# Full-row low pass in C's scores and A's compressed product, batched fronts in D, and a new order of the attention in a hybrid mixer layer

## The chip, the cores and the metric

The kernel runs on one core of one Trainium2 chip. The metric is the device time of one execution in microseconds; times are given as the median of several runs. A core has five engines with queues of their own: TensorE (PE, matrix products; its weight loads are listed as PEld), VectorE (DVE), ScalarE (ACT), GpSimd (POOL) and SyncE (SP, which here only issues DMAs). PSUM has eight banks of 128 rows by 512 numbers of 32 bits, into which PE writes.

## What is computed

One layer: a normalised and modulated input `h` of 1024 tokens by 1024 channels, projections of it, four causal token mixers of four heads of 64 channels each, gated products with `w_br`, a sum over the mixers with gates taken from `h`, an output projection with residual, and a last RMSNorm.

```python
shift, scale, gate = split(silu(c) @ w_ada + b_ada, 3)
h = rms_norm(x, norm_g) * (1 + scale) + shift
(a_q, a_kv, a_g, a_z, b_q, b_k, b_v, b_z,
 c_q, c_k, c_v, c_z, d_q, d_k, d_v, d_z) = split(h @ w_in)
y_a = nsa_attention(a_q, a_kv, a_g, ...)      # compressed, full and window parts
y_b = banded_attention(b_q, b_k, b_v, 128, slopes, sink)
y_c = stick_breaking_attention(c_q, c_k, c_v)
y_d = retention(d_q, d_k, d_v)
for y, z in branches:
    merged += sigmoid(h @ w_merge[i]) * ((y * silu(z)) @ w_br[i])
x = x + gate * (merged @ w_out)
out = rms_norm(x, final_g)
```

For C the score `z` of a query and a key runs over 64 channels, and its weight is `exp(log_sigmoid(z) + suffix)`, with `suffix` the sum of `log_sigmoid(-z)` over the keys between. For D, chunks of 128 tokens have a product of queries and keys times a decay matrix, and a state of 64x64 numbers for each head is carried from chunk to chunk. A's compressed part has 32 keys, each made from a block of 32 tokens.

## The kernel before, in words

**Exact parts.** Most matmuls take operands of a short type (F32R). So that the product keeps its precision, an operand is split in two parts, high and low (`hh`, `hl` of the input, `whi`, `wlo` of weights, `hi`, `lo` of attention weights), and a dense product is three matmuls: `hh·whi`, `hl·whi`, `hh·wlo`. A head has 64 channels, so for C's scores the high and low parts of a query stand one above the other in 128 rows (`q_item`: [hi; lo] for the first head of a pair, [lo; hi] for the second), and the high part of the keys stands twice, in both halves of rows (`ck_item`, L556; the second copy by a DMA on SP). One matmul over 128 rows then gives (q_hi + q_lo)·k_hi. A second one, over the 64 rows of q_hi, adds q_hi·k_lo (`c_units`, L1153 and L1154); the low parts of both heads' keys share one tile `klo`, the first head's in its upper half of rows and the second's in the lower. Matmuls of D's mixer and the transposes are in full 32 bits.

**Stages.** 0 to about 75 us: the norm, the modulation, the first tiles of projections. Then attention by groups: C0a and C0b (C's first two heads, in two parts), D0, C1, D1, A0, A1, B0, B1, to about 600 us. From 600 to 1000 us the merge, whose gate projections are done in Winograd's form (sums and differences `tt` of blocks of `h`, and of weights), and then the output projection with the norms. A group is a row of units. A unit of C is one head and two blocks of 128 queries; a unit of D (`d_units`, L1190) one chunk of 128 tokens for two heads; A and B take a block of queries. Each unit has a `front` (scores, in banks `s`, and what makes weights of them) and a `back` (transposes into banks `t`, the split in `hi` and `lo`, products with values into `y`; `pv_blocks`, L1078). In between run the dense projection items, in banks `d`, which fill PE.

**Buffers.** PSUM: three banks `s`, two `t`, two `d`, one `y`. `sp_pool` has four places of 128x1024 for rows of weights, `t1_pool` two of 128x512, and the weight loads `wst` two. A C front takes two places of `sp_pool`. D's front in the kernel before keeps its products in a place of `t1_pool`.

**What sets the order.** The class `Program` notes every instruction in plain program order with a rank. `SHIFT_PE` and `SHIFT` (L99, L111) add numbers to the ranks of whole parts, named by group and unit, such as ("C1", 2) or ("item", 21). `schedule()` (L256) is then a list schedule of the five engines with durations from `cost()` (L172): each engine takes, of what should be ready, the instruction of lowest rank. `issue()` emits them in that order, which is why nearly all instructions carry line L304 in the trace. The order on each engine is fixed when the program is built; at run time an engine waits until its next instruction's inputs are there.

**In D's front**, for each chunk: two score matmuls with 64 rows (head 0 on rows 0 to 63, head 1 on rows 64 to 127) into two banks, a transpose of the keys, two products with the decay matrix on DVE (128x128), two scalings on ACT, one product of the queries with the decay `xi` on POOL.

Of the kernel before, what the change touches and what calls it, by code (L numbers as in the profile page):

```python
# [10 lines left out]
F32 = mybir.dt.float32  # L11
# [18 lines left out]
# columns of w_in  # L30
# [68 lines left out]
SHIFT_PE = {  # L99
# [7 lines left out]
    ("h1", 7): -10600, ("item", 2): -80, ("item", 4): -11000, ("item", 5): -9200, ("item", 9): 9800, ("item", 11): 0,  # L107
    ("item", 16): -10000, ("item", 21): 9800, ("item", 23): 14100, ("item", 26): 13200, ("item", 27): 19300,
    ("item", 28): 2200, ("item", 30): 12600, ("mod", 5): -11400, ("mod", 6): -9700,
}  # L110
SHIFT = {  # L111
# [8 lines left out]
    ("item", 2): 12700, ("item", 3): 14900, ("item", 4): 10000, ("item", 7): 10200, ("item", 12): -13400, ("item", 13): 9500,  # L120
    ("item", 15): -10000, ("item", 16): 13100, ("item", 18): -8700, ("item", 19): 9600, ("item", 22): 10000,
    ("item", 23): 9800, ("item", 24): 9700, ("item", 25): -10100, ("item", 27): -800, ("item", 29): 12700, ("mod", 4): 10000,
    ("mod", 6): 10100, ("split", 5): 9400, ("x", 4): -10000,
# [4 lines left out]
class Op:  # L128
    __slots__ = ("eng", "calls", "dur", "lat", "preds", "succs", "prio", "start", "step", "size")

    def __init__(self, eng, prio, step):
        self.eng, self.prio, self.step = eng, prio, step
        self.calls, self.dur, self.lat, self.size = [], 0.0, 0.0, 0
        self.preds, self.succs = set(), []


class Program:
    """Instructions are first noted in plain program order, then issued by a list schedule of all engines: each
    engine takes, of what should be ready, the instruction that comes first by rank."""
# [17 lines left out]
    # -- noting  # L157
# [14 lines left out]
    def cost(self, eng, name, out, ins, kw):  # L172
# [16 lines left out]
        if eng == "dve":  # L189
# [4 lines left out]
            if name == "tensor_tensor_reduce":  # L194
                return 77 + n * 1.042
# [10 lines left out]
    def note(self, eng, name, fn, args, kw):  # L206
# [48 lines left out]
    # -- issuing  # L255
    def schedule(self):  # L256
# [6 lines left out]
        engs = ("pe", "act", "dve", "pool", "sp")  # L263
# [8 lines left out]
        dma = warm = 0.0  # L272
        while len(order) < len(ops):
# [5 lines left out]
            op = ops[i]  # L279
            op.start = t  # L280
# [26 lines left out]
    def noted(self, tc, late=0.0):  # L307
        """a part of the program whose instructions are noted, then issued; the other engines come to it later than TensorE"""
# [24 lines left out]
class Pool:  # L333
    """Slots that the tiles of a tag take in turn."""
# [12 lines left out]
class Slots:  # L347
    """Places that tiles take in turn."""
# [10 lines left out]
def hybrid_kernel(ctx: ExitStack, tc: tile.TileContext, x, c, w_ada, b_ada, norm_g, w_in, cmp_pos,  # L359
# [21 lines left out]
    # ------------------------------------------------------------ weights  # L381
# [6 lines left out]
    class Loads:  # L388
        """Loads run two pieces ahead of their splits."""
# [42 lines left out]
    def mtile_weights(it, srcs):  # L432
        """srcs: ((dram view [P, KC, n], n), ...) that make up 128 columns"""
# [33 lines left out]
    def mm3(ps, hi, lo, n0):  # L467
        """ps += h^T-projection of a 128-column weight tile for 512 tokens, in exact parts"""
# [7 lines left out]
    # ------------------------------------------------------------ prologue  # L476
# [12 lines left out]
    vcr = cst.tile([64, P], F32R, name="vcr")  # L489
# [13 lines left out]
    # ---------------------------------------------------- dense items  # L503
# [24 lines left out]
    def half_item(col, full):  # L528
        """the second half of the tokens of an item whose first half is there"""
# [12 lines left out]
    def q_item(col, q0, q1, scale, load=True):  # L542
        """query pair -> stacks [hi; lo] of the first head, [lo; hi] of the second"""
# [12 lines left out]
    def ck_item(col, kk0, kk1, klo, load=True):  # L556
        def evac(ps, n):
# [5 lines left out]
            ve.tensor_tensor(klo()[0:64, sl], ps[0:64], kk0()[0:64, sl].bitcast(F32), ALU.subtract)  # L563
            ve.tensor_tensor(klo()[64:128, sl], ps[64:128], kk1()[64:128, sl].bitcast(F32), ALU.subtract)
# [15 lines left out]
    def v_item(col, vout, tmp, is_d, load=True):  # L580
        """values of a head pair: channel-major projection, turned token-major on chip"""
# [26 lines left out]
    def z_item(col, br, p):  # L608
        """y *= 2 silu(z); all but the first branch of the merge wait in DRAM for their turn"""
# [22 lines left out]
    CK = [(2, 3, 4), (9, 10, 11)]  # L632
# [11 lines left out]
    for p in range(2):  # L644
        it_c.append([q_item(C_Q + P * p, rs(CQ[p][0]), rs(CQ[p][1]), 0.125, False),
                     ck_item(C_K + P * p, rs(CK[p][0]), rs(CK[p][1]), rs(CK[p][2]), False),
                     v_item(C_V + P * p, (lambda p: lambda: R["v2"](CV[p]))(p), Fs[1 + 2 * p], False, False)])
# [54 lines left out]
    # compression of keys and values of A: both at once through block-diagonal weights; the exact parts of the rows stand  # L702
    # side by side as one stationary operand, those of the weights as one moving operand
# [3 lines left out]
    def w1_split(h):  # L707
        """sixteen of the 32 rows of a block, four to a slot"""
# [29 lines left out]
    def cmp_done(g):  # L738
# [29 lines left out]
        te.matmul(pv[0:32, 0:64], lhsT=sg[64:128], rhs=w2t[64:128], start=True, stop=True)  # L768
        kkc, llc = R["q"]["kc"], R["q"]["lc"]
# [18 lines left out]
    # the first tiles grow along with the modulation: one row block of weights after the other  # L788
# [20 lines left out]
    # the second half of the tokens  # L809
# [61 lines left out]
    # pieces follow the order of the items  # L871
# [15 lines left out]
    # ---------------------------------------------------------------- attention  # L887
    with ac:
# [20 lines left out]
        # the compressed keys stand before those of the full part  # L909
# [4 lines left out]
        R["kcs"], R["lcs"] = RAF[:, 0:S + 32], RAF[:, S + 32:2 * S + 64]  # L914
        R["zz"] = RW
# [1018 lines left out]
```

## Time and profile before

| what | value |
|---|---|
| runs of the kernel before | 1148.17, 1146.26, 1146.23 us; median 1146.26 |
| profiled execution: span (it has no other time) | 1143.8 us, 16113 instructions |
| PE busy | 1076.6 us, 94% |
| PEld busy (weight loads, beside PE) | 879.8 us, 77% |
| DVE busy | 841.2 us, 74% |
| ACT busy | 591.6 us, 52% |
| POOL busy | 597.7 us, 52% |

The span runs from the first to the last instruction that the profiler recorded. Matmuls overlap in the records: each has a start and a modelled end, so the cost of one in a run is read from its start to the next start. In the names of a row, `d<-hh,whi` is a matmul into bank `d` of `hh` with weights `whi`; `128*128 128x512` are rows and columns of the stationary operand, then the moving operand. RA, RV, RW and RQ are large tiles that are used as slots for the stacks of queries, keys and values, FA the one for full 32-bit rows. PEclk is the share of full clock that PE was granted.

### The profile page before, as it was taken

What the parts mean: (1) busy time and instruction counts of PE and PEld (TensorE: products, weight loads), DVE (VectorE), ACT (ScalarE), POOL (GpSimd) and SP (SyncE); (2) the same over time, 40 slices, a digit from 0 to 9 for tenths busy, and PEclk for the clock granted to TensorE, in tenths of its full rate; (3) what the DMA queues carried; (4) which work ended last, traced back from release to release, by engine and by line L of the source; (5) the groups of instructions that cost most, each with busy time, mean ns of one, the idle gap of its engine ahead of it and who ended that gap; (6) DMA issues with size and microseconds to landing.
All of it is one profiled execution on the core that took longest, in us unless ns stands there. A gap on an engine that the chain in (4) does not pass through costs nothing. (4 is left out here: it accounts for less than half of the span.)

```text
span 1143.8 us, 16113 instructions
## 1 busy us (share of the span) xinstructions
PE 1076.6 (94%) x5391; PEld 879.8 (77%) x5391; DVE 841.2 (74%) x1777; ACT 591.6 (52%) x1317; POOL 597.7 (52%) x598
## 2 busy tenths in 40 slices
PE   5899999999999999999999589999999999988984
PEld 3777787688888888888878468887778888866763
DVE  6969975887557777767778995666686565678887
ACT  4388863886347666666763333422333333344343
POOL 4683215211535455454455653456666666776775
PEclk9899999999999999999999799999999999998998
DMA  9843102113022010013022023322222332332221
GB/s 300 243 127 84 47 1 52 43 37 56 14 75 55 10 47 29 28 37 76 29 75 69 33 60 95 99 78 65 78 88 56 52 98 73 119 111 87 80 92 74
DMA packets 119591, 85.03 MB, mean 74 GB/s; under 512 B 14428, under 2 KB 107668, under 8 KB 119508
## 3 DMA queue, kind: packets, MB, share of 16 engines
q1 hardware_dynamic: 118352, 80.55, 24.6%
q0 software_dynamic: 1088, 3.43, 0.8%
q8 instruction: 42, 0.69, 0.2%
q14 instruction: 41, 0.34, 0.1%
q10 hardware_dynamic: 68, 0.02, 0.0%
HBM read 72.45 MB, written 8.39 MB: 71 GB/s over the span
## 5 line engine op out<-in xcount | busy, mean ns | idle before, releaser
L304 POOL TENSOR_TENSOR wlo<-wst,whi 128x512 fp32r<-128x512 f32 (+1 forms) x108 | 141.8, 1324 | 176.0 <-ACT whi L304 173.8
L304 PE MATMUL d<-hh,whi 128*128 128x512 f32 x440 | 186.5, 424 | 3.1 <-ACT whi L304 2.5
L304 PE MATMUL d<-hh,wlo 128*128 128x512 f32 x440 | 174.9, 398 | 2.6 <-DVE wlo L304 2.6
L304 PE MATMUL d<-hl,whi 128*128 128x512 f32 x440 | 173.9, 396 | 0.0
L304 ACT ACTIVATE whi<-wst 128x512 fp32r<-128x512 f32 (+2 forms) x121 | 89.1, 736 | 104.7 <-DMA wst<-in_w_merge_dram 41.9
L304 PEld LDWEIGHTS d<-hh,wlo 128*128 128x128 f32 x440 | 83.7, 190 | 21.8 <-DVE wlo L304 3.0
L304 PEld LDWEIGHTS d<-hh,whi 128*128 128x128 f32 x440 | 84.0, 191 | 20.4 <-issue 4.0
L304 ACT ACTIVATE hi<-t 128x512 fp32r<-128x512 f32 (+3 forms) x148 | 74.7, 526 | 46.3 <-PE t L304 38.6
L304 PEld LDWEIGHTS d<-hl,whi 128*128 128x128 f32 x440 | 84.2, 191 | 10.5 <-POOL hl L304 0.2
L304 POOL TENSOR_SCALAR SP<-SP,den,gates 128x640 f32<-128x640 f32 (+7 forms) x64 | 49.7, 786 | 81.4 <-DVE den L304 61.5
L304 DVE TENSOR_TENSOR lo<-t,hi 128x512 fp32r<-128x512 f32 (+2 forms) x132 | 79.9, 621 | 10.5 <-ACT hi L304 9.7
L304 PE MATMUL s<-hl,whi 128*128 128x512 f32 x200 | 79.2, 397 | 3.4 <-DVE hl L304 3.4
L304 PE MATMUL s<-hh,wlo 128*128 128x512 f32 x200 | 79.5, 398 | 1.9 <-DVE wlo L304 1.9
L304 PE MATMUL s<-hh,whi 128*128 128x512 f32 x200 | 80.2, 401 | 0.1
L304 PE MATMUL t<-kbt,SP 128*128 128x128 f32 (+1 forms) x470 | 69.0, 275 | 8.3 <-DMA kbt<-in_kb_dram 7.0
L304 ACT ACTIVATE SP<-SP,mx 128x257 f32<-128x257 f32 (+9 forms) x96 | 62.3, 650 | 22.8 <-DVE mx L304 18.0
L304 ACT ACTIVATE mt<-mt 128x512 f32<-128x512 f32 x56 | 35.0, 625 | 69.9 <-POOL mt L304 50.2
L304 POOL TENSOR_TENSOR acc<-acc,mt 128x512 f32<-128x512 f32 x44 | 67.7, 1539 | 6.1 <-DVE mt L304 6.1
L304 PEld LDWEIGHTS t<-kbt,SP 128*128 128x128 f32 (+1 forms) x470 | 54.7, 141 | 17.9 <-DMA kbt<-in_kb_dram 7.0
L304 POOL TENSOR_TENSOR mt<-mt,mt 128x512 f32<-128x512 f32 x34 | 52.4, 1540 | 12.6 <-DVE mt L304 11.8
L304 PE MATMUL s<-tt,whi 128*128 128x512 f32 x176 | 54.5, 391 | 0.0
L304 PE MATMUL s<-RA,RW 128*128 128x256 f32 (+13 forms) x216 | 49.8, 332 | 0.3 <-DMA RA<-RA 0.3
(360 smaller groups left out, 2961.4 us busy)
## 6 DMA issues: line engine op xcount, KB each, us to landing
wst<-in_w_merge_dram SPq DMA_DIRECT2D x32, 512.0 KB, 4.4
wst<-in_w_in_dram SPq DMA_DIRECT2D x26, 512.0 KB, 3.7
FA<-in_w_ada_dram SPq DMA_DIRECT2D x10, 512.0 KB, 7.5
FA<-in_x_dram SPq DMA_DIRECT2D x8, 512.0 KB, 4.5
pst<-in_w_br_dram SPq DMA_DIRECT2D x32, 128.0 KB, 2.2
ga<-in_w_ada_dram SPq DMA_DIRECT2D x16, 256.0 KB, 3.0
wr<-in_w_out_dram SPq DMA_DIRECT2D x4, 1024.0 KB, 7.5
z<-in_x_dram SPq DMA_DIRECT2D x8, 512.0 KB, 3.5
```

Source lines behind the costliest of these rows:

```text
L304: fn(*args, **kw)
```

## The change

Four things.

1. **C's low pass.** The second matmul of a score takes all 128 rows, q's high and low parts, against the keys' low part, which now has to stand in both halves of rows, in a tile of its own for each head. For the first head pair two more DMAs on SP for each half of the tokens make the second copy. For the second pair the low parts go to a spare slot "f2", and four DMAs on POOL's queue copy them into the slots 2 and 3, which held the first pair's keys. There are 24 such matmuls for each head pair, of 128 to 512 columns. The product q_lo·k_lo is added by this.
2. **A's compressed product.** The matmul with the compressed values `vcr` takes 128 rows in place of 64; rows 64 to 127 of `vcr` are zeroed by a memset on POOL. There are 16, of 256 columns.
3. **D's fronts** are done for four chunks at once, in every fourth unit: eight two-head score matmuls in a row, four transposes, two DVE products of 128x512 in place of eight of 128x128, two ACT instructions in place of eight, one POOL product of 128x512 in place of four. The results stand in two places of `sp_pool` in place of one of `t1_pool`.
4. **The order.** Both tables of numbers are new throughout, and the planner's costs change: other factors for matmuls, 300 ns more for an operation on PE that has a stationary operand of 64 rows or less, and DVE and POOL not at once where both use a port. The order of the merge and the output comes from these costs too. Comments are dropped.

```diff
 SHIFT_PE = {
-    ("A0", 2): 600, ("A0", 4): 100, ("A0", 6): -9300, ("A0", 7): 10000, ("A0", 10): 10500, ("A0", 11): -10000,
+    ('A0', 0): -10000, ('A0', 1): 1967, ('A0', 11): -300, ('A0', 12): -10000, ('A0', 13): 0,
...
             if "rhs" in kw and m.dtype == F32:
-                return max(214.0, n * 1.668)
-            return 2.5 + max(104.5, n * 0.4167)
+                return max(214.0, n * (1.63 if kw["lhsT"].shape[0] <= 64 else 3.33))
+            return max(109.0, n * 0.4427)
...
+            wide = [a for a in ins if a.shape[-1] > 1 and str(a.space) == "SB"]
+            n = 2 - (name in ("tensor_copy", "tensor_scalar") and str(out.space) == "SB")
+            op.port |= eng == "pool" and bool(ins) or eng == "dve" and len(wide) >= n
+            if eng == "pe" and "lhsT" in kw and kw["lhsT"].shape[0] <= 64 and not op.narrow:
+                op.narrow = True
+                op.dur += 300.0
...
+            if op.port:
+                t = max(t, port["dve" if e == "pool" else "pool"])
+                port[e] = t + op.dur
...
-    vcr = cst.tile([64, P], F32R, name="vcr")
+    vcr = cst.tile([P, P], F32R, name="vcr")
...
-    def ck_item(col, kk0, kk1, klo, load=True):
+    def ck_item(col, kk0, kk1, kl0, kl1, both, load=True):
...
-            ve.tensor_tensor(klo()[0:64, sl], ps[0:64], kk0()[0:64, sl].bitcast(F32), ALU.subtract)
-            ve.tensor_tensor(klo()[64:128, sl], ps[64:128], kk1()[64:128, sl].bitcast(F32), ALU.subtract)
+            ve.tensor_tensor(kl0()[0:64, sl], ps[0:64], kk0()[0:64, sl].bitcast(F32), ALU.subtract)
+            ve.tensor_tensor(kl1()[64:128, sl], ps[64:128], kk1()[64:128, sl].bitcast(F32), ALU.subtract)
+            if both:
+                sy.dma_start(kl0()[64:128, sl].bitcast(F32), kl0()[0:64, sl].bitcast(F32))
+                sy.dma_start(kl1()[0:64, sl].bitcast(F32), kl1()[64:128, sl].bitcast(F32))
...
-    CK = [(2, 3, 4), (9, 10, 11)]
+    CK = [(2, 3, 4, 11), (9, 10, "f2", "f2")]
+    CKL = [(4, 11), (2, 3)]
...
-                     v_item(D_V + P * p, lambda: DV3, Fs[2 + p], True)])
+                     v_item(D_V + P * p, lambda: DV3, Fs[1 + 2 * p], True)])
...
+        po.memset(vcr[64:128].bitcast(F32), 0.0)
...
-                        te.matmul(y[:, yc:yc + n], lhsT=v, rhs=hi[:2 * nk, col:col + n], start=f, stop=end)
+                        te.matmul(y[:, yc:yc + n], lhsT=v, rhs=hi[:, col:col + n], start=f, stop=end)
...
-            klo = slot(CK[p][2])
+            klo = [slot(i) for i in CKL[p]]
+            if p == 1:
+                for e in range(2):
+                    for o in (slice(0, 64), slice(64, 128)):
+                        po.dma_start(klo[e][o], slot(CK[p][2])[64 * e:64 * e + 64])
...
-                                te.matmul(ps[:, :n], lhsT=q[hr], rhs=klo[hr, c0:c0 + n], start=False, stop=True)
+                                te.matmul(ps[:, :n], lhsT=q, rhs=klo[e][:, c0:c0 + n], start=False, stop=True)
...
+                    if n % 4:
+                        res["w"] = four["w"]
+                        return
...
-                    for e in range(2):
-                        b = slice(64 * e, 64 * e + 64)
-                        te.matmul(sp[e][:, 0:P], lhsT=DK[b, bl], rhs=DQ[b, bl], start=True, stop=True)
+                    for c in range(4):
+                        for e in range(2):
+                            b = slice(64 * e, 64 * e + 64)
+                            te.matmul(sp[e][:, c * P:(c + 1) * P], lhsT=DK[b, cs[c]], rhs=DQ[b, cs[c]], start=True, stop=True)
```

What the order does is read from the listing of each engine's instructions, before (L304) and changed (L346). The first place is PE, at D0's first fronts, where the scores are `s<-FA`. Before:

```order
L304 MATMUL d_131<-hh,wlo_141 128x512
L304 MATMUL s_132<-FA 128x128
L304 MATMUL s_133<-FA 128x128
L304 MATMUL t_139<-kbt,SP 128x128 x4
L304 MATMUL t_125<-kbt,SP 128x128 x4
L304 MATMUL d_131<-kbt,FA 128x128 x4
L304 MATMUL s_132<-FA 128x128
L304 MATMUL s_133<-FA 128x128
```

The same place changed:

```order
L346 MATMUL d_130<-hh,wlo_137 128x512
L346 MATMUL d_131<-kbt,FA 128x128 x4
L346 MATMUL s_132<-FA 128x128
L346 MATMUL s_133<-FA 128x128
L346 MATMUL s_132<-FA 128x128
L346 MATMUL s_133<-FA 128x128
```

A pair of scores stood between transposes or dense work each time; now four pairs (two are shown) stand in a run.

The second place is POOL behind the first tiles, where splits of weights (`wlo<-wst,whi`) meet the copies of C1's keys (`RA<-FA`) and D0's product (`SP<-FA`; before `t_127<-FA`). Before:

```order
L304 TENSOR_TENSOR wlo_137<-wst_124,whi_136 128x512 x2
L304 TENSOR_TENSOR wlo_141<-wst_138,whi_140 128x512 x2
L304 TENSOR_TENSOR t_127<-FA 128x128 x2
L304 TENSOR_TENSOR t_129<-FA 128x128
L304 TENSOR_SCALAR rs_157<-mv_156 128x2
```

Changed:

```order
L346 TENSOR_TENSOR wlo_137<-wst_124,whi_136 128x512 x2
L346 DMA RA<-FA 64x1024 x2
L346 TENSOR_TENSOR wlo_141<-wst_138,whi_140 128x512 x2
L346 TENSOR_TENSOR SP<-FA 128x512
L346 DMA RA<-FA 64x1024 x2
L346 TENSOR_TENSOR SP<-FA 128x512
L346 TENSOR_SCALAR rs_157<-mv_156 128x2
```

The four copies are new, in two pairs (one for each slot), each ahead of other work of POOL; D0's products are done in two.

The third place is DVE at the start of the merge, where `mt` and `tt` are sums of blocks of the input and `ga` sums for the output's gate. Before:

```order
L304 TENSOR_TENSOR mt_5763<-hh 128x512
L304 TENSOR_TENSOR mt_5766<-hh 128x512
L304 TENSOR_SCALAR ga_5770<-ga_5769,silc 128x128
L304 TENSOR_TENSOR mt_5763<-mt_5763,mt_5764 128x512
L304 SCALAR_TENSOR_TENSOR ga_5770<-ga_5769,silc,ga_5770 128x128
L304 TENSOR_TENSOR mt_5765<-hh,mt_5763 128x512
L304 TENSOR_TENSOR tt<-mt_5763,tt 128x512
```

Changed:

```order
L346 TENSOR_TENSOR mt_5712<-hh 128x512
L346 TENSOR_TENSOR mt_5715<-hh 128x512
L346 TENSOR_TENSOR mt_5712<-mt_5712,mt_5713 128x512
L346 TENSOR_TENSOR mt_5715<-mt_5715,mt_5716 128x512
L346 TENSOR_TENSOR tt<-mt_5712,tt 128x512
L346 TENSOR_TENSOR mt_5714<-hh,mt_5712 128x512
L346 TENSOR_TENSOR tt<-mt_5715,tt 128x512
```

The gate sums are gone from here, and two chains of block sums alternate. The first sum of weights for the next products (`s<-wst`) is the 20th row behind the first one shown before, and the 33rd changed.

## Rows read from the trace of the kernel before

**Rows 1.** The page: busy us, share of the span, instructions of each engine.

```profile
PE 1076.6 (94%) x5391; PEld 879.8 (77%) x5391; DVE 841.2 (74%) x1777; ACT 591.6 (52%) x1317; POOL 597.7 (52%) x598
```

**Rows 2.** Busy time by stage, whole kernel; the first line names the columns.

```profile
core 0: us, PE busy (x) PEld busy (x) DVE busy (x) ACT busy (x) POOL busy (x), PEclk, DMA share, GB/s
75.00:152.00 77.00, 77.00 (x367) 58.04 (x368) 69.57 (x131) 67.02 (x141) 25.08 (x18) 1.00 0.24 65
...
192.00:267.00 75.00, 73.36 (x386) 56.66 (x387) 62.40 (x130) 59.89 (x136) 15.93 (x17) 1.00 0.19 41
267.00:600.00 333.00, 329.82 (x1986) 284.41 (x1985) 235.17 (x814) 206.34 (x553) 160.44 (x239) 1.00 0.17 44
600.00:690.00 90.00, 74.99 (x298) 58.73 (x297) 81.31 (x93) 31.12 (x57) 51.23 (x39) 0.91 0.19 59
```

**Rows 3.** Waits of PE, 75 to 600 us: total us, times, longest.

```profile
PE y L304 <- DVE FA L304: 1.7, 2, 1.3
...
PE y L304 <- DVE yt L304: 0.4, 1, 0.4
```

**Rows 4.** Timeline of PE in C0: start us, us, instruction, count.

```profile
108.36 0.59 PE L304 MATMUL s<-RA,RW 128*128 128x256 f32 x2
108.88 0.50 PE L304 MATMUL d<-hh,whi 128*128 128x512 f32 x1
109.21 0.39 PE L304 MATMUL d<-hl,whi 128*128 128x512 f32 x1
...
111.50 0.81 PE L304 MATMUL s<-RA,RW 128*128 128x512 f32 x2
112.24 0.55 PE L304 MATMUL t<-kbt,SP 128*128 128x128 f32 x3
```

**Rows 5.** Timeline of PE in A: a score of two full-row matmuls.

```profile
488.30 0.46 PE L304 MATMUL s<-RA,RQ 128*128 128x320 f32 x2
488.60 0.39 PE L304 MATMUL d<-hh,whi 128*128 128x512 f32 x1
488.83 0.40 PE L304 MATMUL d<-hl,whi 128*128 128x512 f32 x1
```

**Rows 6.** Busy time in 100 to 125 us, columns as in rows 2.

```profile
100.00:125.00 25.00, 25.00 (x122) 18.92 (x121) 23.70 (x44) 22.48 (x48) 5.07 (x5) 1.00 0.20 54
```

**Rows 7.** Timeline of PE in A: the compressed product and its neighbours.

```profile
486.99 0.28 PE L304 MATMUL y<-lo,RV 128*128 128x256 f32 x1
487.19 0.38 PE L304 MATMUL y<-hi,vcr 64*128 64x256 f32 x1
487.50 0.50 PE L304 MATMUL d<-hh,whi 128*128 128x512 f32 x1
487.84 0.39 PE L304 MATMUL d<-hl,whi 128*128 128x512 f32 x1
```

**Rows 8.** Groups by line and shape: count, busy us, mean ns.

```profile
L304 PE MATMUL y<-hi,vcr 64*128 64x256 f32 x16 | 6.1, 381 | 0.1
```

**Rows 9.** Timeline of PE in D0: one front's scores.

```profile
155.09 0.28 PE L304 MATMUL y<-lo,RA 128*128 128x256 f32 x1
155.29 0.49 PE L304 MATMUL s<-FA 64*128 64x128 f32 x4
155.72 0.50 PE L304 MATMUL d<-hh,whi 128*128 128x512 f32 x1
156.06 0.39 PE L304 MATMUL d<-hl,whi 128*128 128x512 f32 x1
```

**Rows 10.** DMA issues: count, KB each, median us from issue to landing.

```profile
yd<-FA POOLq DMA_DIRECT2D x12, 256.0 KB, 2.4
...
RA<-RA SPq DMA_DIRECT2D x20, 128.0 KB, 2.2
```

**Rows 11.** Waits of PE, 600 to 690 us, columns as in rows 3.

```profile
PE d L304 <- ACT whi L304: 5.4, 1, 5.4
```

More of the change, by code (lines that the diff above doesn't have):

```diff
@@ L99 @@
 SHIFT_PE = {
[7 rows of a table removed]
-    ("h1", 7): -10600, ("item", 2): -80, ("item", 4): -11000, ("item", 5): -9200, ("item", 9): 9800, ("item", 11): 0,
-    ("item", 16): -10000, ("item", 21): 9800, ("item", 23): 14100, ("item", 26): 13200, ("item", 27): 19300,
-    ("item", 28): 2200, ("item", 30): 12600, ("mod", 5): -11400, ("mod", 6): -9700,
[12 rows of a table added]
+    ('first', 0): 300, ('first', 1): 0, ('first', 2): 300, ('first', 4): 9970, ('first', 5): 21923,
[3 rows of a table added]
+    ('h1', 7): 0, ('item', 0): 0, ('item', 10): 0, ('item', 11): 43, ('item', 12): 0,
@@ L110 @@
+    ('item', 13): 100, ('item', 14): -100, ('item', 16): -9900, ('item', 17): 10870,
+    ('item', 19): 9990, ('item', 2): -10000, ('item', 21): 0, ('item', 22): 0, ('item', 26): 633,
+    ('item', 28): 10000, ('item', 30): 9997, ('item', 4): -300, ('item', 5): 9997,
+    ('item', 6): 9960, ('item', 7): 9967, ('item', 9): 2077, ('mod', 0): 0, ('mod', 1): 3000,
+    ('mod', 2): 11000, ('mod', 3): 2900, ('mod', 4): -11000, ('mod', 5): -3, ('mod', 6): 0,
+    ('mod', 7): 7000,
 }
 SHIFT = {
[8 rows of a table removed]
-    ("item", 2): 12700, ("item", 3): 14900, ("item", 4): 10000, ("item", 7): 10200, ("item", 12): -13400, ("item", 13): 9500,
@@ L121 @@
-    ("item", 15): -10000, ("item", 16): 13100, ("item", 18): -8700, ("item", 19): 9600, ("item", 22): 10000,
-    ("item", 23): 9800, ("item", 24): 9700, ("item", 25): -10100, ("item", 27): -800, ("item", 29): 12700, ("mod", 4): 10000,
-    ("mod", 6): 10100, ("split", 5): 9400, ("x", 4): -10000,
[12 rows of a table added]
+    ('D1', 5): 10173, ('D1', 6): 2990, ('ada', 3): -300, ('ada', 4): 10000, ('ada', 7): -30,
[3 rows of a table added]
+    ('item', 1): 10300, ('item', 10): -9910, ('item', 12): 20, ('item', 13): -10320,
+    ('item', 14): -300, ('item', 15): -10997, ('item', 16): 9997, ('item', 18): 0,
@@ new lines @@
+    ('item', 19): 1100, ('item', 2): 0, ('item', 20): 0, ('item', 21): 0, ('item', 22): 273,
+    ('item', 23): 0, ('item', 24): 100, ('item', 25): -10000, ('item', 26): 19676, ('item', 27): 0,
+    ('item', 28): -9700, ('item', 29): -10000, ('item', 3): -3000, ('item', 30): 997,
+    ('item', 4): 130, ('item', 5): 0, ('item', 6): 0, ('item', 7): 0, ('item', 8): -10643,
+    ('item', 9): -10000, ('mod', 1): -11000, ('mod', 3): 0, ('mod', 4): 1000, ('mod', 5): -10800,
+    ('mod', 6): -10980, ('mod', 7): -10000, ('split', 0): 0, ('split', 1): -10000,
@@ L124 @@
+    ('split', 2): -3000, ('split', 3): -10000, ('split', 4): -200, ('split', 6): 10300,
+    ('split', 7): 21169, ('x', 4): 19990, ('x', 5): 10300, ('x', 6): 0, ('x', 7): -10000,
 }
@@ L128 @@
 class Op:
-    __slots__ = ("eng", "calls", "dur", "lat", "preds", "succs", "prio", "start", "step", "size")
+    __slots__ = ("eng", "calls", "dur", "lat", "preds", "succs", "prio", "start", "step", "size", "port", "narrow")
     def __init__(self, eng, prio, step):
@@ L133, in __init__ @@
         self.calls, self.dur, self.lat, self.size = [], 0.0, 0.0, 0
+        self.port = self.narrow = False
         self.preds, self.succs = set(), []
@@ L194, in cost @@
             if name == "tensor_tensor_reduce":
-                return 77 + n * 1.042
+                return 77 + n * 1.042 + 60 * max(0, cols - 1)
+            if name == "tensor_tensor_scan":
+                return 69 + n * 2.11
             fast = not psum and name in ("tensor_scalar", "tensor_copy")
@@ L272, in schedule @@
         dma = warm = 0.0
+        port = {"pool": 0.0, "dve": 0.0}
         while len(order) < len(ops):
@@ L1196, in d_units, with front @@
             units = []
+            four = {}
             for n in range(NT):
                 bl = slice(n * P, (n + 1) * P)
-                def front(res, n=n, bl=bl):
+                def front(res, n=n):
+                    if n % 4:
+                        res["w"] = four["w"]
+                        return
+                    cs = [slice(c * P, (c + 1) * P) for c in range(n, n + 4)]
                     sp = [pools["s"].tile([P, 512], F32, name=f"ds{uid()}", tag="s") for _ in range(2)]
@@ L1213, in front @@
-                    po.tensor_tensor(w[:, 384:512], DQ[:, bl], xi, ALU.mult)
-                    res["w"] = w
+                    for c in range(4):
+                        te.transpose(t[:, c * P:(c + 1) * P], DK[:, cs[c]], ident)
+                    s = sp_pool.tile([P, S], F32, name=f"dsw{uid()}", tag="sp").rearrange("p (e c j) -> p e c j", e=2, j=P)
+                    w = sp_pool.tile([P, S], F32, name=f"dw{uid()}", tag="sp").rearrange("p (v c j) -> p v c j", v=2, j=P)
+                    t3 = t.rearrange("p (c j) -> p c j", j=P)
@@ L1216, in back @@
+                    res["w"] = four["w"] = s, w
                 def back(res, n=n, bl=bl):
-                    w = res["w"]
+                    s, w = res["w"]
                     v = DV3[:, n, :]
@@ L1221, in back @@
                     if n > 0:
-                        te.matmul(y[:, 0:P], lhsT=w[:, 384:512], rhs=rbd, start=True, stop=False)
+                        te.matmul(y[:, 0:P], lhsT=w[:, 1, n % 4], rhs=rbd, start=True, stop=False)
                     for e in range(2):
-                        te.matmul(y[:, 64 * e:64 * e + 64], lhsT=w[:, e * P:(e + 1) * P], rhs=v[:, 64 * e:64 * e + 64],
+                        te.matmul(y[:, 64 * e:64 * e + 64], lhsT=s[:, e, n % 4], rhs=v[:, 64 * e:64 * e + 64],
                                   start=(n == 0), stop=(n == 0 or e == 1))
@@ L1228, in back @@
                         yield [u]
-                        te.matmul(u[:, 0:P], lhsT=w[:, 256:384], rhs=v, start=True, stop=True)
+                        te.matmul(u[:, 0:P], lhsT=w[:, 0, n % 4], rhs=v, start=True, stop=True)
                         for e in range(2):
```

15 lines of the change are left out of this document (8 added, 7 removed), and 43 rows, old and new, of tables (SHIFT, SHIFT_PE).

## The prediction

> **What bounds the kernel now.** I read four views in this order: busy time by engine, busy time by stage, what TensorE waited for, and TensorE's timeline around the instructions that the diff edits.
>
> TensorE (PE) is busy for 1076.6 us, 94% [rows 1]. By stage this isn't uniform [rows 2]: from 75 to 600 us, where the diff's edits lie, PE is busy nearly throughout (77.00 of 77.00, 73.36 of 75.00 and 329.82 of 333.00 us in the three stretches shown), while from 600 to 690 us, where attention hands over to the merge, it has 74.99 of 90.00. The idle time between 75 and 600 us is made of six groups of waits, the largest 1.7 us and the smallest 0.4, 4.7 us in all [rows 3]. So there a microsecond of PE work saved is a microsecond of time, until another engine binds. That engine is VectorE (DVE): 69.57 us in the first C stretch and 62.40 of 75.00 in the second [rows 2].
>
> **C's low pass.** A score of C is a pair of matmuls, 128 rows and then 64. From start to start a pair of 512 columns takes 112.24 − 111.50 = 0.74 us, a pair of 256 takes 0.52, and the dense 512-column matmul behind it 109.21 − 108.88 = 0.33 [rows 4]. A dense matmul in a run takes 488.83 − 488.60 = 0.23, two 320-column matmuls, both of 128 rows, together 0.30, and the matmul behind them the plain 0.23 [rows 5]. At 0.23 for 512 columns and 0.12 for 256, the 64-row pass costs 0.28 us beyond its columns at both sizes, and its follower 0.10. Each head pair has 24 such pairs of matmuls (2 heads, 8 blocks of queries, half of them in two pieces); in some 19 of 24 a dense matmul follows. So 24 × 0.28 + 19 × 0.10 = 8.6 us for each head pair, 17.2 in all. The widened pass has the same columns, so it costs what any full matmul costs.
>
> What of it reaches the end is set by DVE. The listing shows that the dense work among these scores stays: 198 dense 512-column matmuls between C0's first and last score before, 201 now, and C1's 141 + 48 of 268 columns become 162 + 6, the same columns within 1%. So the stretches can shrink only as far as DVE's work allows. The densest I find DVE in a C stretch is 23.70 of 25.00 us, 95% [rows 6]. At that share C0's 69.57 us of DVE fill 73.2 us, a gain of **3.8** of the 8.6. C1's 62.40 us fill 65.7 at 95%, so all 8.6 would fit; at C0's present share (69.57/77.00 = 90.4%) they fill 69.0 and 6.0 is gained. I take the middle, **7.3**. Bounds for both stretches together: 0 + 6.0 and 17.2.
>
> **A's compressed product.** The 64-row matmul starts 0.20 us behind its neighbour in place of 0.12, takes 487.50 − 487.19 = 0.31 for 256 columns in place of 0.12, and its follower 0.34 in place of 0.23 [rows 7]: 0.08 + 0.19 + 0.11 = 0.38 us. There are 16 [rows 8], all between 267 and 600 us, where DVE has 235.17 us of 333.00 [rows 2] and can't bind: **6.1 us**. The new memset of 64 rows is one POOL instruction, hidden.
>
> **D's fronts.** A two-head pair standing alone costs 0.08 ahead, 155.72 − 155.29 = 0.43 itself and 0.11 on its follower [rows 9], 0.62 us. Four in a run pay the edges once: 4 × 0.43 + 0.19 = 1.91 against 2.48, and there are four batches: **2.3 us**. Lower bound 0 (the edges aren't saved); upper bound 4.8, if three of four pairs in a run also halve. The transposes are the same. DVE's, ScalarE's and POOL's instructions become fewer and larger; none binds in D, so 0. The batch takes two of the four score places, so C1's first score starts after D0's fourth back.
>
> **What is added.** SP gets two more copies of 64x512 for each half of C0's keys; 2.2 us from issue to landing [rows 10]. C0's first low pass waits that much longer, and weight loads queue behind on SP; loads run two pieces ahead of use, so 0, at worst 3 us. POOL gets four DMAs of 256 KB for C1's keys; such a one lands after 2.4 us [rows 10]. They wait for C0's last low passes, with splits of weights and D's product queued behind on POOL, which is busy 15.93 of 75.00 us in C1 [rows 2]. Between C0's last score and C1's first stand 60 dense matmuls, 60 × 0.23 = 14 us, and the products with values besides: cover enough. 0; if a split came late, up to 3 us.
>
> **The order.** Elsewhere the tables reshuffle what PE has to do anyway. In the handover to the merge PE's largest wait is 5.4 us for one weight part of ScalarE [rows 11]; the new DVE order takes the gate sums out from between the sums of blocks, but the first sum of weights stands 33 rows behind the first of the stage in place of 20. I take 0, ±5 us; for the prologue 0, ±3.
>
> **Sum.** 3.8 + 7.3 + 6.1 + 2.3 = 19.5 us. The profiled execution has only its span, 1143.8, which becomes 1124.3; the median of the runs shown is 1146.26, 2.4 us more, and becomes **1126.8**.
>
> **A rule against it.** PE shows in D that 64-row matmuls on the two halves run as one pair of 0.43 us, and in C that a lone 64-row pass costs 0.28 more than its columns [rows 4, 9]. The Trainium skill ("TensorEngine Tiling (Array Packing)", Theoretical Speedup) has row tiling make contractions of up to 64 rows up to twice as fast, which speaks for narrow passes; its Key Properties say that a change of tiling mode drains TensorE, which fits the rows of C, where the mode changes twice for each score. By the first, widening gains nothing (rival 3); by the second, the sum above stands.
>
> **The rivals.**
> 1. *DVE binds both C stretches.* For: 90.4% of C0 now, PE waiting on DVE's score tiles at the stage's edges. Against: C1 has 12.6 us free. Then C yields nothing, 6.1 + 2.3 = 8.4 is left: 1137.9 us (1134 to 1142). Chance 0.20.
> 2. *All of PE's saving reaches the end, and the handover gains.* 17.2 + 6.1 + 2.3 = 25.6, and some 5 us of the 15.0 idle from 600 to 690: 1115.7 us (1109 to 1119). For: the new order can move DVE's work out of C0. Against: the 95%. Chance 0.14.
> 3. *The change doesn't do what it says.* A widened pass costs as much as the narrow one, because the 0.28 us is the price of changing the stationary rows of a score and not of 64 rows. Rows 5 speak against it: two full passes show no such price. 1146 us. Chance 0.05.
> 4. *Slower.* The new order starves PE in C0 and C1: a DVE result that PE needs comes behind others' work, and PE shows 83% as in the handover (74.99 of 90.00, its granted clock 0.91 there) [rows 2]. It decides once the waits pass the saving, 25.6 us in the 152 us of the two stretches; at 83% there 152 × 0.17 = 26 us of waits, and at a mean clock of 0.91 another 126 × 0.09 = 11: 1146.3 − 25.6 + 37 = 1158 us. For: DVE has only 7.4 us free in C0. Against: PE waits 4.7 us in all of 75 to 600 now [rows 3], and the dense work is still there to fill. Chance 0.09.
>
> **How the numbers follow.** The forecast has 0.52, its own range 1119 to 1134: C's bounds (6.0 to 17.2 against 11.1 taken), D's, and ±5 for the order. The range of 8 in 10 takes in most of rivals 1 and 2 and leaves out the ends: **1112 to 1142**. About 0.2%, 2.3 us, is what a measurement of this kernel tells from no change. Faster: 0.52 + 0.20 + 0.14 = 0.86; same, 0.05 (rival 3); slower, 0.09.
>
> **What would show it.** Right: the low pass in C stands at mean durations of full matmuls, the pair of 512 at 0.46 us from start to start; the product with compressed values at 0.12; runs of eight scores in D; PE's waits in the C0 stretch grow by some 5 us, on DVE; 267 to 600 shorter by 7. Wrong: PE without waits in C0 (rival 2), C stretches as long as before with PE idle (rival 1), pairs still at 0.74 (rival 3), or waits of tens of microseconds and a granted clock under 1 between 75 and 267 us (rival 4).

## The result, and the profile after

The changed kernel takes 1114.24 us (median; 1112.57 to 1115.1), the kernel before 1146.54 beside it: a ratio of 0.9717, 95% interval 0.9703 to 0.973, or 32.3 us less. The forecast was 1126.8 us with a range of 1112 to 1142. The direction and the range held; the measured time is 12.6 us below the central value and 2.2 us above the lower end of the range.

The page of the changed kernel, profiled execution of 1112.57 us: busy time by engine, and PE and its granted clock over 40 slices.

```profile
span 1110.8 us, 16056 instructions
...
PE 1043.6 (94%) x5391; PEld 877.6 (79%) x5391; DVE 840.1 (76%) x1753; ACT 589.7 (53%) x1293; POOL 600.2 (54%) x591
...
PE   5799999999999999999999699999999999995985
...
PEclk9799999999999999999999899999999999997998
```

The share of PE is the same 94% as in [rows 1], with the same 5391 matmuls: 33.0 us of PE's busy time are gone and 33.0 us of the span. Idle time of PE is 67.2 us in both.

The stages, cut near C0's first score, D0's first, and C1's first and last; behind them, the cut at 570 lies 12 us before the last product of attention weights with values (at 581.8), and the cut at 600 in [rows 2] lies 2 us before it (at 601.7). Columns as in [rows 2]:

```profile
0.00:83.00 83.00, 60.91 (x285) 48.24 (x286) 58.81 (x121) 44.42 (x79) 50.86 (x60) 0.90 0.76 219
83.00:158.00 75.00, 74.21 (x392) 61.71 (x392) 69.52 (x132) 67.14 (x141) 24.25 (x21) 1.00 0.36 84
158.00:185.00 27.00, 25.42 (x183) 21.73 (x182) 15.57 (x52) 11.31 (x24) 10.01 (x13) 1.00 0.14 38
185.00:250.00 65.00, 64.86 (x374) 55.65 (x373) 59.45 (x137) 57.19 (x130) 15.72 (x19) 1.00 0.10 20
...
570.00:660.00 90.00, 77.17 (x318) 61.10 (x318) 77.74 (x91) 32.02 (x61) 52.02 (x40) 0.92 0.18 56
660.00:970.00 310.00, 310.00 (x1377) 256.84 (x1376) 202.60 (x286) 112.81 (x205) 187.61 (x143) 1.00 0.28 81
970.00:1110.80 140.80, 114.72 (x500) 92.74 (x498) 122.35 (x143) 62.11 (x120) 100.37 (x67) 0.92 0.28 100
```

Before, C0's first score came at 74.6 us, now at 83.5; PE's idle time up to there went from 16.9 us (75.00 − 58.09) to 22.1. So the prologue lost some 5 us. The C0 stretch has both engines nearly full: PE 74.21 of 75.00, DVE 69.52. PE's wait for the banks of scores on DVE, which was to grow by some 5 us, is 0.2 us from 70 to 260 us. The merge, from 660 to 970 us, has no idle time at all on PE, where before it had 2.3 of 310. In all, attention ends 19.9 us earlier (581.8 in place of 601.7), and what follows takes 529.0 us in place of 542.1, 13.1 less.

The matmuls do what was forecast. A score of C and its neighbours, then a batch of D and its neighbours, on PE's timeline:

```profile
109.39 0.39 PE L346 MATMUL d<-hh,wlo 128*128 128x512 f32 x1
109.62 0.46 PE L346 MATMUL s<-RA,RW 128*128 128x320 f32 x2
109.91 0.39 PE L346 MATMUL d<-hh,whi 128*128 128x512 f32 x1
110.14 0.40 PE L346 MATMUL d<-hl,whi 128*128 128x512 f32 x1
...
157.21 0.60 PE L346 MATMUL d<-kbt,FA 128*128 128x128 f32 x4
157.74 1.16 PE L346 MATMUL s<-FA 64*128 64x128 f32 x16
159.17 0.39 PE L346 MATMUL y<-hi,RA 128*128 128x256 f32 x1 [0.27 <-DVE FA L346]
159.40 0.28 PE L346 MATMUL y<-lo,RA 128*128 128x256 f32 x1
```

The score pair takes 0.29 us for two of 320 columns and its follower 0.23, as in [rows 5] and not as in [rows 4]. The first run of eight scores of D takes 1.43 us to the next start, 0.27 of it a wait; the other three runs take 1.17, 1.16 and 1.09. The compressed product, by shape, has a mean of 317 ns for 381 in [rows 8]:

```profile
L346 PE MATMUL y<-hi,vcr 128*128 128x256 f32 x16 | 5.1, 317 | 0.3 <-DVE hi L346 0.3
```

### The profile page after: what moved, and what is told of

It reads as the page before. It is cut to its first block, busy times and chain, and to the rows that moved or that the text cites. A ratio compares the mean times of both kernels' runs of the same rounds, so it can differ in the third digit from the quotient of the medians.

```text
span 1110.8 us, 16056 instructions
## 1 busy us (share of the span) xinstructions
PE 1043.6 (94%) x5391; PEld 877.6 (79%) x5391; DVE 840.1 (76%) x1753; ACT 589.7 (53%) x1293; POOL 600.2 (54%) x591
## 4 chain that ended last, share of the span: by engine, by line
PE 57%; DVE 10%; issue 3%; ACT 2%; POOL 1%; POOLq 0%; ACTq 0%; DVEq 0%
PE d L346 21%; PE s L346 18%; PE t L346 12%; PE y L346 7%; DVE mt L346 4%; DVE acc L346 1%; DVE wlo L346 1%; DVE hl L346 1%; DVE hl L369 1%; DVE tt L346 0%; DVE SP L346 0%; POOL wlo L346 0%; DVE z L346 0%; POOL mt L346 0%; ACT whi L346 0%
## 5 line engine op out<-in xcount | busy, mean ns | idle before, releaser
L346 POOL TENSOR_TENSOR wlo<-wst,whi 128x512 fp32r<-128x512 f32 (+1 forms) x108 | 141.1, 1317 | 154.6 <-ACT whi L346 140.2
L346 PE MATMUL d<-hh,whi 128*128 128x512 f32 x440 | 182.4, 414 | 16.2 <-ACT whi L346 12.6
L346 PE MATMUL d<-hh,wlo 128*128 128x512 f32 x440 | 174.5, 397 | 1.2 <-POOL wlo L346 1.2
L346 PE MATMUL d<-hl,whi 128*128 128x512 f32 x440 | 173.9, 396 | 0.2 <-POOL hl L346 0.2
L346 ACT ACTIVATE whi<-wst 128x512 fp32r<-128x512 f32 (+2 forms) x121 | 89.0, 737 | 117.7 <-DMA wst<-in_w_merge_dram 35.2
L346 PEld LDWEIGHTS d<-hh,whi 128*128 128x128 f32 x440 | 84.0, 191 | 29.6 <-ACT whi L346 13.5
L346 PEld LDWEIGHTS d<-hh,wlo 128*128 128x128 f32 x440 | 83.4, 190 | 20.9 <-POOL wlo L346 1.6
L346 POOL TENSOR_SCALAR SP<-SP,den,gates 128x640 f32<-128x640 f32 (+7 forms) x64 | 49.8, 787 | 86.7 <-DVE den L346 49.5
L346 PEld LDWEIGHTS d<-hl,whi 128*128 128x128 f32 x440 | 84.2, 191 | 12.0 <-POOL hl L346 0.7
L346 DVE TENSOR_TENSOR lo<-t,hi 128x512 fp32r<-128x512 f32 (+2 forms) x132 | 80.5, 624 | 15.7 <-ACT hi L346 14.8
L346 ACT ACTIVATE hi<-t 128x512 fp32r<-128x512 f32 (+3 forms) x148 | 75.2, 526 | 32.2 <-PE t L346 23.5
L346 PE MATMUL s<-hh,whi 128*128 128x512 f32 x200 | 79.3, 396 | 1.0 <-ACT whi L346 1.0
L346 PE MATMUL s<-hh,wlo 128*128 128x512 f32 x200 | 78.5, 393 | 1.8 <-DVE wlo L346 1.8
L346 POOL TENSOR_TENSOR acc<-acc,mt 128x512 f32<-128x512 f32 x44 | 68.1, 1547 | 19.8 <-DVE mt L346 18.9
L346 PE MATMUL s<-hl,whi 128*128 128x512 f32 x200 | 78.1, 392 | 0.0
L346 ACT ACTIVATE SP<-SP,mx 128x257 f32<-128x257 f32 (+9 forms) x96 | 62.3, 651 | 28.7 <-DVE mx L346 22.9
L346 PE MATMUL t<-kbt,SP 128*128 128x128 f32 (+1 forms) x470 | 69.4, 273 | 8.6 <-DMA kbt<-in_kb_dram 6.9
L346 ACT ACTIVATE mt<-mt 128x512 f32<-128x512 f32 x56 | 35.1, 628 | 65.8 <-POOL mt L346 48.4
L346 PEld LDWEIGHTS t<-kbt,SP 128*128 128x128 f32 (+1 forms) x470 | 55.5, 141 | 16.0 <-DMA kbt<-in_kb_dram 6.9
L346 PE MATMUL s<-tt,whi 128*128 128x512 f32 x176 | 55.7, 398 | 2.9 <-ACT whi L346 2.9
L346 POOL TENSOR_TENSOR mt<-mt,mt 128x512 f32<-128x512 f32 x34 | 49.9, 1467 | 9.0 <-DVE mt L346 7.8
L346 ACT ACTIVATE t<-t 128x512 f32<-128x512 f32 (+5 forms) x97 | 50.2, 524 | 1.3
```

Of the source, the lines that this page charges most:

```text
L346: fn(*args, **kw)
```

## The experiments

Times are medians, with the kernel before measured beside each set. The question for the first four: how much of the change's 32.3 us are the wide matmuls, and where is the rest?

**e1, C's low pass alone, in the old order.** The old order of attention is written out as a list, so no instruction moves.

```diff
-te.matmul(ps[:, :n], lhsT=q[hr], rhs=klo[hr, c0:c0 + n], start=False, stop=True)
+te.matmul(ps[:, :n], lhsT=q, rhs=klo[:, c0:c0 + n], start=False, stop=True)
```

> The kernel before, every instruction in its place (the old order is written out), with one edit: C's low pass takes all 128 rows of the query stack against the one shared tile of low parts. No copies are needed for that: the added product is q_lo of this head with k_lo of this or the other head, which is as small as the product that the kernel leaves out anyway. Theory 1 (the prediction: VectorE lets 3.8 + 7.3 us through): 11.1 us less, 1135.4, and PE's waits on DVE from 75 to 267 us grow by some 6 us. Theory 2 (PE's whole price reaches the end): 17.2 us less, 1129.3, and the waits stay as they were. Theory 3 (the two C stretches are as long as before): 1146.5.

1136.79 us against 1146.36, ratio 0.9915 (0.99 to 0.993): 9.6 us less. That is theory 1, and a little less than it. PE's stretches in C0 and C1 in this run, columns as in [rows 2]:

```profile
75.00:150.00 75.00, 72.68 (x372) 57.85 (x373) 69.38 (x131) 67.45 (x143) 25.57 (x18) 1.00 0.26 67
190.00:259.00 69.00, 66.25 (x382) 55.35 (x381) 61.06 (x129) 59.03 (x134) 15.94 (x16) 1.00 0.20 44
```

Its largest wait from 70 to 267 us, columns as in [rows 3]:

```profile
PE s L321 <- DVE SP L321: 2.7, 5, 1.0
```

PE, which had no idle time in C0 and 1.64 us in C1 [rows 2], has 2.3 us in C0 now and 2.75 in C1, and its wait for the banks of scores on DVE goes from 0.7 to 2.7 us. Summed over the steps from the start of one full-row matmul to the start of a full-row matmul right behind it, beyond what the columns take (0.443 ns each, at least 0.109 us a matmul), the stretch from 75 to 275 us had 9.1 us before and has 17.0 here: part of the price has turned into short waits. DVE is then at 92.5% of C0 (69.38 of 75.00).

**e2, the compressed product alone, in the old order.**

```diff
-rhs=hi[:2 * nk, col:col + n]
+rhs=hi[:, col:col + n]     # vcr with 128 rows, 64 of them zero
```

> The kernel before, every instruction in its place, with one edit: A's compressed product takes 128 rows, the lower 64 zeroed by a memset. Prediction: 16 x 0.38 = 6.1 us less, 1140.4; the matmul 0.12 us from start to start in place of 0.31. A theory by which the price belongs to the change of stationary rows and not to 64 rows: 1146.5, no change.

1141.25 us, ratio 0.9952 (0.9935 to 0.9969): 5.1 us less of the 6.1. The theory by which the price belongs to any change of stationary rows, and not to 64 of them, falls.

**e3, C's low pass narrow again, in the new order.**

```diff
-te.matmul(ps[:, :n], lhsT=q, rhs=klo[e][:, c0:c0 + n], ...)
+te.matmul(ps[:, :n], lhsT=q[64 * e:64 * e + 64], rhs=klo[e][64 * e:64 * e + 64, c0:c0 + n], ...)
```

> The changed kernel, every instruction in its new place, C's low pass back at 64 rows (the copies stay, unused halves and all). Theory 1 (VectorE hides part of PE's price): 11.1 us more, 1125.3. Theory 2 (PE's whole price reaches the end): 17.2 us more, 1131.4.

1129.11 us, 14.9 more than the change: between the theories, nearer to the second. In the new order most of PE's price reaches the end; in the old order 9.6. From its first score to its last, C0 takes 76.2 us here and 69.6 in the change, C1 70.3 and 62.1: 6.6 and 8.2 us gained, where the old order (before and e1) gains 3.0 and 5.5. The new order has moved DVE's work out of C0. From its first score to its last, before, here and in the change, columns as in [rows 2]:

```profile
74.63:149.71 75.08, 75.08 (x355) 56.47 (x356) 67.65 (x127) 65.19 (x139) 25.45 (x18) 1.00 0.25 67
84.40:160.61 76.21, 76.06 (x362) 57.39 (x361) 64.68 (x125) 64.08 (x133) 21.33 (x19) 1.00 0.29 74
83.47:153.10 69.63, 68.84 (x363) 57.30 (x361) 64.43 (x125) 63.14 (x133) 21.65 (x19) 1.00 0.34 81
```

DVE was busy for 67.65 of 75.08 us before, and is for 64.68 of 76.21 with the same narrow pass in the new order.

**e4, the old planner for the merge and the output only.**

```diff
 def noted(self, tc, late=0.0):
+    self.old = True     # old costs, old ties, no exclusion of DVE and POOL
```

> The changed kernel with the planner's old costs, ties and no DVE/POOL exclusion for the merge and the output only; the attention's order is untouched. In the traces the time from the end of attention to the end of the span is 13.5 us shorter with the change. Theory A (the planner's costs gave this): 13.5 us more, 1127.7. Theory B (it comes from the state in which attention leaves the engines and buffers): within 3 us of 1114.2. The prediction had 0 +- 5 for this part.

1128.04 us, 13.8 more: theory A, and the term that the prediction had put at 0. PE works through 660 to 970 us of the change without a gap; with the old plan (span 1125.1) it has 2.4 us of gaps again in that part, and 28.4 behind it in place of 26.1:

```profile
660.00:980.00 320.00, 317.60 (x1395) 260.29 (x1394) 203.59 (x287) 112.43 (x207) 189.40 (x144) 1.00 0.28 80
980.00:1125.00 145.00, 116.56 (x491) 91.72 (x489) 115.25 (x141) 60.52 (x118) 94.99 (x67) 0.93 0.25 92
```

That is 4.7 us of gaps more than in the change; most of the 13.8 is in waits so short that they lie under the modelled ends of the matmuls, so that PE counts as busy. Between the starts of matmuls behind attention, steps that are longer than their columns take by less than 0.5 us add up to 18.2 us with the old plan and to 9.7 in the change. What PE waits for changes too: the waits that the profile lists from 560 us on and puts down to DVE come to 20.2 us with the old plan and 8.0 in the change, those put down to ScalarE to 9.0 and 16.5. Two that go, with the old plan, columns as in [rows 3]:

```profile
PE d L352 <- DVE wlo L352: 4.2, 2, 2.1
...
PE t L352 <- DVE wlo L352: 3.0, 3, 1.2
```

**e5 and e6, a dose of DVE work in C**, in e1's kernel and in the change, the order kept in each.

```diff
 ve.scalar_tensor_tensor(l, ps[:, :n], 0.0, l, op0=ALU.max, op1=ALU.add)
+ve.tensor_scalar(l, l, 1.0, None, op0=ALU.mult)
```

> The kernel of e1 (before, old order written out, C's low pass wide: 1136.8) with one more DVE instruction for each of C's 48 score pieces: a multiplication of the row piece by 1.0 behind the maximum, same places for all else. It leaves the result as it is. By the like rows of the trace each takes some 0.3 us or a little over, so 13 to 17 us of DVE work over the two C stretches. Theory 1 (with the wide pass DVE binds the C stretches in the old order): most of it is paid, 8 us or more, 1145. Theory 2 (PE binds there still): 0 to 3 us, 1138.

> The same added DVE instruction in the changed kernel, its new order kept. If the new order made room on DVE in the C stretches (theory of e3, where 14.9 of 17.2 us of the price came through): half or less of the added work is paid, under 7 us, 1114 to 1121. If DVE binds there as in the old order: 8 us or more, 1122.

e5 takes 1160.83 us, 24.0 more than e1; e6 1132.09, 17.9 more than the change. The dose was larger than expected, so the limits in microseconds don't fit; the shares do. DVE's group of these instructions (one of the 49 is another) in e5, then in e6:

```profile
L321 DVE TENSOR_SCALAR t<-t 128x512 f32<-128x512 f32 (+5 forms) x49 | 21.1, 431 | 1.7
```

```profile
L346 DVE TENSOR_SCALAR t<-t 128x512 f32<-128x512 f32 (+5 forms) x49 | 23.0, 469 | 1.6
```

PE's largest wait, for the banks of scores, from 70 to 290 us, in e5, then in e6:

```profile
PE s L321 <- DVE SP L321: 14.7, 21, 2.5
```

```profile
PE s L346 <- DVE SP L346: 7.4, 14, 1.9
```

In the old order all of the dose is paid, and a little more (24.0 of 21.1); in the new order 17.9 of 23.0. So in both orders C's stretches have little room for more DVE work once PE's price is gone, the new order some 5 us, about the difference between e3 and e1. The expectation that under half would be paid in the new order missed. That DVE is the limit is not fully shown by this: with the dose it is busy for 93% of C0 and 90% of C1 (first score to last) in e5, and for 95% and 94% in e6. The added instruction also lengthens the chain of each score; that share was not separated.

**e7, the change without copies of the keys.** The wide pass reads one shared tile as in e1, in the new order.

> The changed kernel in its new order without any copy of C's low keys: as in e1 the wide pass reads one shared tile with both heads' low parts, so the four POOL and four SP transfers and the spare slot go; the added product is as small as the one left out. If the copies are covered, as the prediction had it (0, at worst 3 + 3 us): within 2 us of 1114.2. If C's first scores or POOL's splits wait for them: 3 to 6 us less, 1108 to 1111.

1111.70 us, ratio 0.9705 (0.9683 to 0.9728): 2.5 us below the change, with intervals that overlap. In the traces attention ends at 581.9 us without the copies and at 581.8 with them, so the copies are covered.

**e8, the old attention order with everything but D's batches.** e1, e2 and the new plan of the merge in one kernel.

> The kernel before in its old attention order, written out, with C's low pass and A's compressed product wide, and the planner's new costs for the merge and the output. D's fronts stay single. If the terms add up: 1146.4 - 9.6 (e1) - 5.1 (e2) - 13.8 (e4) = 1117.9, and the batched fronts of D with the new attention order are worth 3.7 us. If the new attention order is worth more (theory that it makes the room for DVE and saves 5 us of C alone), the same sum must come out lower for it; if the terms overlap, the run is slower than 1118, up to 1124.

1120.08 us: 2.2 above 1117.9, the sum of the terms, which thus nearly add up. What is left to the change, D's batches and the new order of attention, is 5.8 us net, the loss in the prologue and C's larger gain in the new order included.

**e9 and e10, which of the planner's costs**, in the kernel before, for the merge and the output.

```diff
 if op.port:
     t = max(t, port["dve" if e == "pool" else "pool"])   # e9: with this alone; e10: all the rest alone
     port[e] = t + op.dur
```

> The kernel before, attention untouched; for the merge and the output the planner keeps its old costs and ties and only learns that DVE and POOL don't run at once where both use their port. The whole of the new costs was worth 13.8 us here (e4), 11.3 by e8. Theory A (the exclusion is what makes the plan fit the chip): 8 us or more less, 1138 or below. Theory B (the other costs do it: the matmul of 109 and 0.4427, the reductions): within 3 us of 1146.

> The complement of e9: the kernel before with all the new costs and ties for the merge and the output, but without the exclusion of DVE and POOL. Theory A: within 4 us of 1146. Theory B: 8 us or more less, 1138 or below. If both e9 and e10 gain half, the gain is the sum of small things.

e9 takes 1131.14 us against 1146.72, 15.6 less; its ratio, 0.9878 (0.9851 to 0.9904), makes it 14.0, for one of its four runs took 1137.01. e10 takes 1165.67, ratio 1.0177 (1.0156 to 1.0197), 19 us more. The exclusion alone brings the whole gain of the merge; the other costs without it do harm, which was not expected. With either set of costs the plan that has the exclusion is the faster one, by 14 to 16 us with the old costs and by some 30 with the new (19 more without it, e10; 11 to 14 less with it, e8 and e4). But these are four plans, and e10 shows how far a plan can move by costs alone; that the exclusion helps because it is true of the chip is argued, not shown.

**e11, the old numbers for the prologue.** In both tables, the entries of the prologue's parts (mod, ada, split, x, first, h0, h1) from the kernel before, the rest as in e7.

> The kernel of e7 (the change without copies of keys, 1111.7) with the old numbers for the prologue's parts in both tables. In the trace of the change PE has 60.9 us of work in the 83 us to C's first score; before it had 58.1 in 75. If this is a loss of the new order, the run wins some 4 to 5 us, 1107. If the work done there is paid back later, or the old numbers don't fit beside the new ones: 1110 to 1116.

1153.66 us, 42 more than e7. PE starves in the stretch around C1, and its granted clock falls there:

```profile
200.00:290.00 90.00, 74.58 (x373) 61.31 (x372) 57.54 (x140) 58.64 (x129) 18.65 (x23) 0.86 0.15 34
```

PE is at 83% of these 90 us with a mean granted clock of 0.86, and DVE isn't full either (57.54 us): the order is at fault. Beside e7, the time is some 8 us longer up to C0's first score, 8 from there to D0's first, and 28 from there to C1's last. Numbers of two tables don't mix, so the prologue's loss of 5 us is not shown to be one that could be had back.

**e12, e7 with the exclusion alone in the merge.**

> The kernel of e7 (the change without copies of keys, new attention order, 1111.7) with the planner's old costs plus the exclusion alone for the merge and the output. In the old kernel that was worth 15.6 us (e9) where all the new costs were worth 13.8 (e4) or 11.3 (e8). If these add up, 2 to 4 us less than e7: 1108 to 1110. If the two plans are equal within what can be told: 1110 to 1114.

1113.34 us, ratio 0.9715 (0.9702 to 0.9729). So in the changed kernel too the exclusion alone keeps the gain; the two plans of the merge can't be told apart here, and no version was found that is clearly faster than the change.

## Why the prediction was right, and where it was wrong

The direction and the range held, and the range in part by luck. The forecast's sum, 19.5 us, lay in the stages up to the end of attention, which give 19.9; but there C and D gave more than forecast, A less, and the prologue took some 5 us back. The 13.1 us behind attention were not in the sum. Without the prologue's loss the time would have been some 1109 us, below the range.

**PE bounds 75 to 600 us, and 64-row matmuls cost beyond their columns.** Right: e1 and e2 take time out with no instruction moved, and the rows after show pairs at the plain price. The Trainium skill ("TensorEngine Tiling (Array Packing)", Key Properties) has a change of tiling mode drain TensorE; the trace agrees, 0.28 us on the narrow pass and 0.10 on the next matmul [rows 4], and nothing on either after. The speed-up of row tiles that the Trainium skill states on the same page (Theoretical Speedup) did not show in C, whose narrow pass stands alone; pairs of D on both halves of rows do run together [rows 9].

**"What of it reaches the end is set by DVE"**: 3.8 + 7.3 = 11.1. The mechanism has good support in the order for which it was worked out: 9.6 in e1, with PE's new waits on DVE, and a dose of DVE work that is paid in full. For the changed kernel the term was too low: 14.9 (e3), of it 6.6 in C0 for the 3.8 forecast and 8.2 in C1 for 7.3. The step that failed is that it took C0's DVE work as it was before, 69.57 us, though the order is new: the change has some 3 us less of it between C0's first and last score (64.43 for 67.65), so PE is hardly held up there by DVE. It wasn't DVE's limit of 95% that was wrong: DVE is at 92.5% of that stretch.

**A's product**: 6.1 forecast, 5.1 measured (e2). **D's fronts**: 2.3 forecast; no run did them alone. By the timeline a batch takes a mean of 1.21 us and some 0.2 at its edges, against 4 × 0.62 = 2.48: four batches save 4.3 by this estimate, near the upper bound of 4.8. The pairs do get shorter in a run. **The copies**: 0 forecast, 0 by the traces of e7. **The prologue**: 0 ± 3 forecast, some 5 us lost; PE's wait for ScalarE before its transposes there went from 2.1 to 7.1 us.

**"The order … I take 0, ±5 us"** is the step that failed by most. It was looked at in the handover alone, by the DVE rows there, and the prediction took the rest of the merge and the output as reshuffled work. The plan of these two came from the changed costs and was worth 13.8 us (e4), 11.3 by e8's sum, and by e9 one rule is enough for it, that DVE and POOL don't run at once where both use their port. Counted by the columns that PE has done since attention, 2.5 us are gained in the handover (the first 80 us or so), 5.1 in the next 300, 2.9 from there to PE's last matmuls, and some 2.7 behind them. The trace before had shown such a collision in a row that the prediction didn't use: two DVE sums of 128x512 that lasted 7.14 us while POOL worked beside them. That row of DVE, then the two of POOL, on the timeline of the kernel before:

```profile
608.34 7.14 DVE L304 TENSOR_TENSOR mt<-hh 128x512 f32<-128x512 f32 x2 [1.41 <-POOL FA L304]
```

```profile
609.20 2.54 POOL L304 TENSOR_TENSOR mt<-hl 128x512 f32<-128x512 f32 x2
611.70 2.52 POOL L304 TENSOR_TENSOR wlo<-wst,whi 128x512 fp32r<-128x512 f32 x2
```

A DVE sum of the same size next to it took 0.68 us, so the pair lost nearly 6 us. The Trainium skill ("SBUF — State Buffer", Who interferes with whom) says that a DVE instruction with two SBUF inputs contends with a GpSimd instruction that reads SBUF, for a pair of ports that is an exclusive lock; the row agrees, 7.14 us for 2 × 0.68. But the price of such collisions is not what the new plan saves. The same pair takes as long in the changed kernel:

```profile
588.44 7.13 DVE L346 TENSOR_TENSOR mt<-hh 128x512 f32<-128x512 f32 x2 [1.40 <-POOL FA L346]
```

One group of DVE in the merge fell by a third, as the next two rows show, before and after; others rose, such as all eight `mt<-hh` from 11.7 to 15.5 us.

```profile
L304 DVE TENSOR_TENSOR wst<-s,wst 128x512 f32<-128x512 f32 x14 | 19.9, 1423 | 1.3
```

```profile
L346 DVE TENSOR_TENSOR wst<-s,wst 128x512 f32<-128x512 f32 x14 | 13.3, 950 | 0.3
```

Behind attention DVE is busy for 394.0 us before, 397.7 in the change and 403.6 in e9, so the faster plans have no less DVE time. What fell is PE's waiting for DVE (20.2 to 8.0 us, e4). A plan that believes that both engines run at once puts things behind DVE that come late; that reading fits these numbers, and no run shows it instruction by instruction.

**The sum, mended**: 14.9 (e3) + 5.1 (e2) + 4.3 (D, an estimate from the trace) + 13.8 (e4) − some 5 (prologue) = 33, against 32.3 measured. The terms come from different kernels, so that they add up this closely is partly luck.

**The rivals.** The second, 1115.7, came nearest in time and was half right: most of C's saving got through, for the reason that it gave, DVE's work moved out of C0; but of its 5 us in the handover 2.5 came, and the larger part of the gain lies behind it, in the merge and the output. The first (DVE binds, and C yields nothing) didn't happen in either order, though in the old one nearly half of C's price is held back. The third fell with e2. The fourth, starved C stretches with a lower clock, didn't happen to the change, but e11 shows it for another order: 83% of PE and 1153.7 us. That this is near the 1158 worked out is luck: the waits were to lie in C0 and C1, but e11 kept PE at 97% from 90 to 170 us and had lost 8 us before.

## What to carry to other kernels

When a matmul of half the rows stands alone between full ones, price it by starts, not by columns: here widening it, with zeros or with a product too small to matter, took some 0.3 us off each (14.9 us for 48, 5.1 for 16), and 0.2 where DVE left less room (9.6 for 48). When a list schedule fills several engines, a rule about which can't run together may be worth as much as the largest single edit (13.8 us here beside 14.9), and costs mended without it made the plan worse. And if a change touches a planner's costs, look at every stage that the planner orders, not at those that the rest of the diff names.

## What was not expected of the hardware

A multiplication of a 128-row piece by a constant, in place on DVE, has a mean of 431 to 469 ns for 128 to 512 columns where the like rows seemed to promise 0.3 us, and the 256-column ones differ between orders (295 and 515 ns). A run of eight two-head scores of D takes 1.09 to 1.43 us: in a run a pair takes 0.27 to 0.36 us, less than the 0.43 of a lone one [rows 9].
